# Four equal value groups of 388 columns become 512, 264, 512 and 264 in a two-layer encoder kernel

## The chip, the cores and the metric

The kernel runs on one core of a Trainium2 chip. The metric is the device time of one launch in microseconds. A core has five engines that run side by side and meet at semaphores: TensorE (PE in the profile, its weight loads as PEld) multiplies matrices into PSUM; ScalarE (ACT) and VectorE (DVE) work elementwise; GpSimd (POOL) and SyncE (SP) here mostly issue DMAs. Sixteen DMA engines move data between HBM, where the inputs lie, and SBUF, the memory that the engines read.

## What is computed

The reference is a trunk of two layers over 256 positions of width 2048. In each layer one projection feeds three groups of heads, whose gated outputs go through one output projection, a residual and a layer norm:

```python
h = x @ w_in
a_q, a_k, a_v, a_z, b_q, b_k, b_v, b_z, b_lr, m_q, m_z = jnp.split(h, cuts, axis=-1)
y_a = chunk_band_attention(heads_a(a_q), heads_a(a_k), heads_a(a_v), rel_table)   # 8 heads of 128
gate_logit = (b_lr @ gate_w + gate_b)
o_b = gla_chunk_recurrence(heads_k(b_q), heads_k(b_k), b_v, log_g)                # 4 heads, gated linear attention
y_m = memory_attention(heads_m(m_q), mk, mv)                                      # 4 heads over 256 memory tokens
y = jnp.concatenate([y_a * silu(a_z), y_b * silu(b_z), y_m * silu(m_z)], axis=-1)
return layer_norm(DEEPNORM_ALPHA * x + y @ w_out, ln_g, ln_b)
```

All inputs and outputs are float32. The change is in the part of `x @ w_in` that gives `b_lr` (16 columns), `b_v` (512) and `a_v` (1024): together 1552 columns, which the kernel calls the values.

## The kernel before

**Products.** To keep float32 accuracy at the matmul's faster format, each operand is split into a rounded part "hi" and a remainder "lo", and a product is three matmuls: hi x hi, lo x hi, hi x lo (`as_products`, L286). ScalarE makes hi by a cast (L124), VectorE makes lo by a subtraction (L125), both in `parts` (L122).

**Groups and pieces.** The projection is done in groups of columns. `as_group` (L294) takes one group of n columns: it has 2048 rows of weights, cut into 8 pieces of 2 x 128 rows. For each piece, `piece` (L136) issues the load of the raw weights into one of four buffers, makes hi and lo in one of four buffers each, and then 12 matmuls use it (2 blocks of rows, 2 halves of the positions, 3 products). They add into an accumulator in PSUM, of which there are two. So the cast of a piece can start when TensorE has finished the piece four before it, and a load can be issued when the lo part of the piece four before it has been made.

**Orders.** TensorE and SyncE run in the order in which the program is written (`manual_schedule`, L49). On ScalarE, VectorE and GpSimd the order is planned when the kernel is built, and `parts` of the weights comes first there (`high_priority(AHEAD)`, L138). All weight loads are issued by SyncE, each in its turn: an issue that has to wait holds up all that stand behind it.

**Background work.** Heads are generators that do a few small steps between the pieces. After each piece the program calls `tick` (L52) with n/512, so time is counted in pieces of 512 columns; a step that asked for 6 ticks comes when 6 have passed. GLA's steps are in `gla` (L334), those of the attention heads in `a_head` (L563), which also loads a table of biases two heads ahead (L565).

**Around the change.** In each layer the groups come in this order: queries and keys of GLA (`G_BQK`, L856), values 0 and 1 (L882, L886), in layer 0 the load of the residual input `xn`, 256 x 2048 float32 (L888), the loads of two bias tables (L893), values 2, queries and keys of attention heads 0 to 3, values 3, queries and keys of heads 4 to 7, and then the memory queries, the gates and the output projection. The four value groups have 388 columns each. They lie in `w388`, of shape (layers, 4, 8, 128, 776): for each group and piece, a partition's two rows of 388 columns lie side by side, so that a load reads 3104 bytes in one run per partition. The result goes by a copy on ScalarE (L870) into `asv`, 128 x 2 x 1552; the first 16 columns are copied on into `lr` (L884) for GLA's first step.

Other groups are loaded in two halves of 256 columns from two places; `piece` then gets a list, and issues one DMA for each entry (L144 to L147).

Of the kernel before, what the change touches and what calls it, by code (L numbers as in the profile page):

```python
# [36 lines left out]
def hybrid_trunk_kernel(  # L37
# [7 lines left out]
    pe, dve, act, pool, sp = nc.tensor, nc.vector, nc.scalar, nc.gpsimd, nc.sync  # L45
# [6 lines left out]
    def tick(share=1.0):  # L52

        now[0] += share
        for e in [e for e in side if e[1] <= now[0]]:
            side.remove(e)
            after = next(e[0], None)
            if after is not None:
                side.append((e[0], now[0] + after))
            else:  # L60
                done.add(e[0])
        while True:
            while waiting and len(active) < (3 if all(g in done for g in linear) else 2):
                active.append((waiting.pop(0), 0))
            due = [e for e in active if e[1] <= now[0]]
            if not due:
                return
            active.remove(due[0])
            g = due[0][0]
            after = next(g, None)  # L70
            if after is not None:
                active.append((g, now[0] + after))
                return
            done.add(g)

    def finish(gens):
        while not all(g in done for g in gens):
            tick()
# [18 lines left out]
    def nm(s):  # L97
        uid[0] += 1
        return f"{s}_{uid[0]}"
# [22 lines left out]
    def parts(hi, lo, src):  # L122

        act.copy(hi, src)  # L124
        dve.tensor_tensor(lo, src, hi.bitcast(F32), op=ALU.subtract)  # L125

    def load_quarter(src):

        with tc.high_priority(AHEAD):
            raw = wp.tile([P, 4, T], F32, name=nm("raw"), tag="raw")  # L130
            x = operand()
            sp.dma_start(raw, src)
            parts(x[0], x[1], raw)
        return x

    def piece(src, n, kp=2, home=None):  # L136

        with tc.high_priority(AHEAD):  # L138
            raw = wp.tile([P, kp, n], F32, name=nm("raw"), tag="raw")
            if home is None:  # L140
                hi, lo = (wp.tile([P, kp, n], F32R, name=nm(w), tag=w) for w in ("wh", "wl"))
            else:
                hi, lo = home
            if isinstance(src, list):  # L144
                w = n // len(src)
                for i, part in enumerate(src):
                    sp.dma_start(raw[:, :, i * w:(i + 1) * w], part.rearrange("p (k n) -> p k n", k=kp))  # L147
            else:
                sp.dma_start(raw.rearrange("p k n -> p (k n)"), src)
            parts(hi, lo, raw)  # L150
        return hi, lo
# [110 lines left out]
    def ws_half(src, xq):  # L262

        acc = psd.tile([P, 2, 2, T], F32, name=nm("acc"), tag="acc")
        for pc in range(4):
            wh, wl = piece(src[pc], 256, 4)
            xh, _, both = xq[pc]
            for j in range(4):
                for b in range(2):
                    mm(acc[:, b].rearrange("p h t -> p (h t)"), wh[:, j, b * P:(b + 1) * P], both[:, j], pc == j == 0, False)  # L270
                for b in range(2):
                    mm(acc[:, b, 1], wl[:, j, b * P:(b + 1) * P], xh[:, j], False, pc == j == 3)
            tick()
        return acc
# [11 lines left out]
    def as_products(o, t, xq, w, kt, kk, first=0):  # L286
        wh, wl = w
        xh, xl, _ = xq[kt // 4]
        j, ts = kt % 4, slice(t * P, (t + 1) * P)
        mm(o, xh[:, j, ts], wh[:, kk], kt == first, False)  # L290
        mm(o, xl[:, j, ts], wh[:, kk], False, False)
        mm(o, xh[:, j, ts], wl[:, kk], False, kt == 15)

    def as_group(src, xq, n, kp=2, first=None, need={}):  # L294

        acc = psd.tile([P, 2, 512], F32, name=nm("acc"), tag="acc")
        for pc in range(16 // kp):
            if first is not None and pc % 2 == 0:
                xq.append(load_quarter(first[pc // 2]))
            finish(need.get(pc, ()))  # L300
            w = piece(src[pc], n, kp)
            for kk in range(kp):
                for t in range(2):
                    as_products(acc[:, t, :n], t, xq, w, pc * kp + kk, kk)
            tick(n / 512)
        return acc
# [365 lines left out]
    def wo_pieces(l, n):  # L672

        if n < 3:
            return [w512[l, G_WO + n, pc] for pc in range(8)]
        return [[w256[l, i, pc // 2][:, pc % 2 * 512:pc % 2 * 512 + 512] for i in range(2)] for pc in range(8)]
# [141 lines left out]
    for l in range(L):  # L818
        def halves(g):
            return [[w512[l, g, h * 4 + pc // 2][:, pc % 2 * 512:pc % 2 * 512 + 512] for h in range(2)] for pc in range(8)]  # L820
# [11 lines left out]
        xq = []  # L832
# [6 lines left out]
        else:  # L839
# [4 lines left out]
            raw = hd.tile([P, 4, T], F32, name=nm("qk"), tag="qk", bufs=4)  # L844
# [5 lines left out]
        raw = hd.tile([P, 4, T], F32, name=nm("qk"), tag="qk", bufs=4)  # L850
# [15 lines left out]
        asv = per.tile([P, 2, 1552], F32, name=nm("asv"), tag="asv")  # L866

        def values(i):
            acc = as_group(w388[l, i], xq, 388)
            act.copy(asv[:, :, i * 388:(i + 1) * 388], acc[:, :, :388])  # L870

        def heads(g):
            t = hd.tile([P, 4, T], F32, name=nm("qk"), tag="qk", bufs=4)
            for i, a, b in ws_group(w512[l, g], xq):
                total(t[:, i:i + 2], a, b)
            return t
# [3 lines left out]
        lr = hd.tile([P, 2, P], F32R, name=nm("lr"), tag="qe")  # L880
        pool.memset(lr.bitcast(F32), 0.0)
        values(0)  # L882
        for i in (0, 32):
            act.copy(lr[:, :, i:i + 16], asv[:, :, :16])  # L884
        dve.tensor_tensor(lr[:, :, 16:32], asv[:, :, :16], lr[:, :, :16].bitcast(F32), op=ALU.subtract)
        values(1)  # L886
        if l == 0:
            sp.dma_start(res, xn.rearrange("(t p) d -> p t d", p=P))  # L888
# [15 lines left out]
        for half in range(2):  # L904
            values(2 + half)
            q = hd.tile([P, 4, T], F32, name=nm("qk"), tag="qk", bufs=4)
            laid = staged(G_AQ0 if half == 0 else G_AQ1, xq, yraw[3], lambda src, at, q=q: act.copy(at(q), src))
            k = heads(G_AK0 if half == 0 else G_AK1)
            finish(laid)
            gens.append([a_head(half * 4 + h, load_bias, bias, q[:, h], k[:, h], asv, yraw[1 + half][:, h]) for h in range(4)])  # L910
            waiting.extend(gens[-1])
# [6 lines left out]
        acc = as_group(halves(G_BZ), xq, 512)  # L918
# [6 lines left out]
        for i, g in ((1, G_AZ0), (2, G_AZ1), (3, G_MZ)):  # L925
            acc = as_group(halves(g), xq, 512)
# [20 lines left out]
        for n in range(WO_N):  # L947
# [3 lines left out]
            src = wo_pieces(l, n)  # L951
            if last and n == WO_N - 1:


                accs = [psd.tile([P, 2, 512], F32, name=nm("acc"), tag="acc")[:, 0], bank()]
                rest = bank()[:, :256]
                both = [operand()[2].rearrange("p (h k) n -> p h k n", h=2),
                        per.tile([P, 2, 2, 512], F32R, name=nm("late"), tag="asv")]
                homes = {pc: (x[:, 0], x[:, 1]) for pc, x in zip((2, 3), both)}
                for i, pc in enumerate((4, 5)):  # L960
                    homes[pc] = [per.tile([P, 2, 512], F32R, name=nm("late"), tag=f"yr{2 * i + k}") for k in range(2)]
                ws = [piece(src[pc], 512, 2, homes.get(pc)) for pc in range(8)]

                def products(o, t, kts, cs=slice(0, 512), first=0):
                    for kt in kts:
                        as_products(o, t, yq, [w[:, :, cs] for w in ws[kt // 2]], kt, kt % 2, first)

                products(accs[0], 0, range(16))

                def more(i):  # L970
                    if i == 0:
                        products(accs[1], 1, range(12))
                        products(accs[1][:, :256], 1, range(12, 16), slice(0, 256))
                    else:
                        products(rest, 1, range(12, 16), slice(256, 512), 12)

                norm_last(accs, rest, stats, gb, rows, more)
                break
# [4 lines left out]
            for m, pc in order:  # L983
                finish(need.pop(pc, ()))
                w = piece(wo_pieces(l, m)[pc], 512)
# [103 lines left out]
```

## Time and profile before

| | us |
|---|---|
| median of 3 runs | 907.38 (907.1 to 908.11) |
| the profiled execution | 907.3 |
| its span, first to last instruction | 905.5 |
| TensorE busy | 898.8 |
| VectorE busy | 605.4 |
| ScalarE busy | 480.3 |
| GpSimd busy | 176.0 |

The span is 1.8 us shorter than the time of its own execution, the rest lying before the first and after the last instruction. The mean clock granted to TensorE is 0.999 of full speed.

In rows of instructions the profile gives the line, the engine, the operation, the tiles it writes and reads, shapes (partitions x elements), a count, the busy time, the mean of one in ns, and the idle time of the engine before them with what ended it. A row in order of time starts with the start and the length in us; neighbours of the same kind are merged, with their count behind the x. SPq is SyncE's queue of DMA issues. Rows by stretch give, for a window of time, its length, the busy time of PE, PEld, DVE, ACT and POOL, the granted clock, the mean busy share of the DMA engines and GB/s. A row of DMA issues gives count, size of one and the median time from issue to landing.

### The profile page before, as it was taken

The page shows a single profiled execution, that of the slowest core. Times are in us where ns is not written, and L with a number is a line of the kernel's source. Part 1 is how long each engine was busy: PE and PEld are TensorE (multiplying, and loading weights), DVE is VectorE, ACT ScalarE, POOL GpSimd, SP SyncE. Part 2 cuts the span into 40 slices and gives each one's busy share as a digit, 9 for nine tenths or more (in the row PEclk, how much of TensorE's full clock was granted, in tenths as well). Part 3 has the DMA queues.
Part 4 walks back from the last instruction along what each step waited for, and adds up shares of the span by engine and source line. Part 5 has one row for each costly group of instructions (what it writes and reads, how often), then busy time and mean ns, then how long its engine had stood idle before and what let it go on. Part 6 is the DMA issues. An engine that isn't in the chain of part 4 may idle for free.

```text
span 905.5 us, 13967 instructions
## 1 busy us (share of the span) xinstructions
PE 898.8 (99%) x4926; PEld 773.8 (85%) x4926; DVE 605.4 (67%) x878; ACT 480.3 (53%) x695; POOL 176.0 (19%) x329
## 2 busy tenths in 40 slices
PE   9999999999999999999999999999999999999997
PEld 8889998998888888888888899889888888888885
DVE  6765478757566676565587676885756586766766
ACT  6654475474544656433466445754745365744440
POOL 0002002015043543200000220021141433334000
PEclk9999999999999999999999999999999999999999
DMA  9977876668787988776775686666696879889752
GB/s 313 319 214 216 299 219 194 182 205 268 216 245 206 275 260 274 225 263 188 232 250 168 202 245 204 198 194 202 192 287 195 261 209 277 253 232 280 232 164 93
DMA packets 131512, 207.16 MB, mean 229 GB/s; under 512 B 14313, under 2 KB 99689, under 8 KB 131185
## 3 DMA queue, kind: packets, MB, share of 16 engines
q1 hardware_dynamic: 117744, 173.28, 61.3%
q0 software_dynamic: 13408, 32.59, 13.1%
q8 instruction: 38, 0.62, 0.3%
q10 hardware_dynamic: 288, 0.39, 0.1%
q14 instruction: 34, 0.27, 0.1%
HBM read 189.93 MB, written 16.25 MB: 228 GB/s over the span
## 4 chain that ended last, share of the span: by engine, by line
PE 99%; DMA 0%; DVE 0%; ACT 0%; issue 0%
PE acc L102 90%; PE bk L102 8%; PE bk L648 0%; DMA raw<-w 0%; PE bk L419 0%; ACT res L804 0%; DVE stats L789 0%; PE bk L366 0%; DVE res L788 0%; ACT wh L124 0%; DVE res L740 0%; DVE mvt L743 0%; PE bk L792 0%; ACT nparts L124 0%; DVE rs_u L751 0%
## 5 line engine op out<-in xcount | busy, mean ns | idle before, releaser
L102 PE MATMUL acc<-wh,x 128*128 128x512 f32 (+2 forms) x2196 | 656.2, 380 | 0.2 <-ACT wh L124 0.2
L125 DVE TENSOR_TENSOR wl<-raw,wh 128x1024 fp32r<-128x1024 f32 (+3 forms) x321 | 368.0, 1151 | 190.2 <-ACT wh L124 188.5
L124 ACT CAST wh<-raw 128x1024 fp32r<-128x1024 f32 (+3 forms) x321 | 318.8, 995 | 320.2 <-PE acc L102 256.4
L102 PEld LDWEIGHTS acc<-wh,x 128*128 128x128 f32 x2196 | 405.5, 188 | 63.4 <-ACT wh L124 0.5
L102 PE MATMUL acc<-wl,x 128*128 128x512 f32 (+2 forms) x1098 | 414.7, 378 | 0.0
L102 PEld LDWEIGHTS acc<-wl,x 128*128 128x128 f32 x1098 | 205.9, 188 | 34.0 <-DVE wl L125 0.4
L556 POOL DMA_DIRECT2D home<-sc x58 | 32.5, 561 | 494.3 <-DVE sc L554 483.9
L102 PE MATMUL acc<-x,wh 128*128 128x512 f32 x288 | 91.1, 398 | 0.0
L102 PEld LDWEIGHTS acc<-x,wl 128*128 128x128 f32 x288 | 54.1, 188 | 12.6
L559 POOL DMA_DIRECT2D pT<-home x96 | 52.6, 554 | 41.4 <-DMA home<-sc 26.7
L102 PE MATMUL acc<-x,wl 128*128 128x256 f32 x288 | 56.7, 278 | 0.0
L102 PEld LDWEIGHTS acc<-x,wh 128*128 128x128 f32 x288 | 44.8, 189 | 1.3 <-ACT wh L124 0.2
L559 POOL DMA_DIRECT2D zT<-home x48 | 26.2, 553 | 32.8 <-DMA home<-sc 17.6
L559 POOL DMA_DIRECT2D yr<-home x48 | 26.1, 551 | 16.2 <-DMA home<-sc 7.9
L554 DVE STREAM_TRANSPOSE sc<-sc 128x512 f32<-128x512 f32 (+1 forms) x36 | 22.6, 642 | 1.9 <-ACT sc L931 1.4
L578 ACT ACTIVATE sc<-sc,mx 128x128 f32<-128x128 f32 (+1 forms) x32 | 14.4, 449 | 17.2 <-DVE mx L576 17.2
L538 DVE TENSOR_TENSOR sc<-zT,yr 128x256 f32<-128x256 f32 x24 | 8.9, 415 | 21.3 <-DMA zT<-home 21.3
L408 ACT ACTIVATE sc<-sc 128x512 f32<-128x512 f32 x12 | 7.6, 633 | 14.9 <-DVE sc L406 14.9
L124 ACT CAST x<-sc 128x512 fp32r<-128x512 f32 x20 | 11.8, 617 | 7.0 <-DVE sc L538 5.7
L571 DVE SCALAR_TENSOR_TENSOR sc<-bk,bias 128x384 f32<-128x384 f32 x16 | 8.7, 543 | 9.5 <-PE bk L102 9.5
L554 DVE STREAM_TRANSPOSE sc<-acc 128x512 f32<-128x512 f32 x18 | 11.8, 693 | 3.6 <-PE acc L102 2.8
L559 POOL DMA_DIRECT2D qk<-home x24 | 13.1, 553 | 5.0 <-DMA home<-sc 5.0
(211 smaller groups left out, 587.5 us busy)
## 6 DMA issues: line engine op xcount, KB each, us to landing
raw<-w SPq DMA_DIRECT2D x323, 256.0 KB, 4.2
raw<-w SPq DMA_DIRECT2D x94, 512.0 KB, 4.9
raw<-w SPq DMA_DIRECT2D x64, 388.0 KB, 3.5
home<-sc POOLq DMA_DIRECT2D x42, 256.0 KB, 4.4
bias<-relw SPq DMA_DIRECT2D x16, 192.0 KB, 4.6
yr<-home POOLq DMA_DIRECT2D x48, 64.0 KB, 4.7
home<-sc POOLq DMA_DIRECT2D x16, 192.0 KB, 3.2
pT<-home POOLq DMA_DIRECT2D x64, 48.0 KB, 4.2
```

Of the source, the lines that this page charges most:

```text
L102: pe.matmul(o, l, r, start=start, stop=stop, skip_group_check=True)
L124: act.copy(hi, src)
L125: dve.tensor_tensor(lo, src, hi.bitcast(F32), op=ALU.subtract)
L408: act.activation(dd, dd, AF.Abs)
L538: dve.tensor_tensor(o, z, r, op=ALU.mult)
L554: dve.transpose(blocks.rearrange("p b (g j) -> p g b j", j=32), src.rearrange("p (g b j) -> p g b j", b=4, j=32))
L556: pool.dma_start(homes[-1], blocks)
L559: pool.dma_start(dst[b * 32:(b + 1) * 32], home[:, b].rearrange("(a i) n -> i a n", a=4))
L571: dve.scalar_tensor_tensor(s, pb[:, :384], SCALE, bias[h], op0=ALU.mult, op1=ALU.add)
L578: act.activation(s[:, own[t]], s[:, own[t]], AF.Exp, bias=mx[:, t:t + 1], accum_out=zs[:, t:t + 1])
```

## The change

The 1552 columns of values are computed in groups of 512, 264, 512 and 264 columns instead of four of 388. The arrays in HBM stay as they are. Groups 0 and 1 (and 2 and 3) share the columns of two neighbouring arrays: the wide one takes all 388 columns of the first and 124 of the second, with two DMAs a piece, and the narrow one takes the other 264 of the second, with one. The runs of these loads are 1552, 496 and 1056 bytes, two per partition, instead of one of 3104. `piece` now takes lists whose entries have different widths. The number of matmuls, casts and subtractions stays; their widths change. `tick` gets 512/512 and 264/512 in place of 388/512.

```diff
             if isinstance(src, list):
-                w = n // len(src)
-                for i, part in enumerate(src):
-                    sp.dma_start(raw[:, :, i * w:(i + 1) * w], part.rearrange("p (k n) -> p k n", k=kp))
+                at = 0
+                for part in src:
+                    if len(part.shape) == 2:
+                        part = part.rearrange("p (k n) -> p k n", k=kp)
+                    sp.dma_start(raw[:, :, at:at + part.shape[2]], part)
+                    at += part.shape[2]
...
         def values(i):
-            acc = as_group(w388[l, i], xq, 388)
-            act.copy(asv[:, :, i * 388:(i + 1) * 388], acc[:, :, :388])
+            def part(j, pc, c0, c1):
+                return w388[l, j, pc].rearrange("p (k n) -> p k n", k=2)[:, :, c0:c1]
+
+            j, n = i // 2 * 2, (512, 264)[i % 2]
+            src = [[part(j + 1, pc, 124, 388)] if i % 2 else [part(j, pc, 0, 388), part(j + 1, pc, 0, 124)] for pc in range(8)]
+            acc = as_group(src, xq, n)
+            c0 = j * 388 + i % 2 * 512
+            act.copy(asv[:, :, c0:c0 + n], acc[:, :, :n])
```

## The prediction

> **What bounds the kernel now.** I read the first page for the busy engine and the chain that ended last, then the list of waits, then the order of time of TensorE, ScalarE, VectorE and SyncE around the value groups, and last the DMA share there.
>
> ```profile
> span 905.5 us, 13967 instructions
> PE 898.8 (99%) x4926; PEld 773.8 (85%) x4926; DVE 605.4 (67%) x878; ACT 480.3 (53%) x695; POOL 176.0 (19%) x329
> PE 99%; DMA 0%; DVE 0%; ACT 0%; issue 0%
> ACT wh L124 <- PE acc L102: 256.4, 184, 4.0
> ACT wh L124 <- DMA raw<-w: 22.5, 24, 4.2
> PEld bk L102 <- issue: 2.2, 8, 0.4
> ```
>
> TensorE is busy 99% of the span and is 99% of the chain: every nanosecond added to or taken from its stream shows in the time. The casts of the weights on ScalarE mostly wait for TensorE to give a buffer back (256.4 us), seldom for a load (22.5 us in 24 waits); so loads run ahead. The longest of those few, 4.2 us, is the place that matters below.
>
> I write V0 to V3 for the four value groups and V1.3 for piece 3 of V1, counting pieces from 0. There are four buffers for each of raw, hi and lo. So the cast of a piece starts when TensorE has finished the piece four before it, and a load is issued when VectorE has made the lo part of the piece four before it.
>
> **The matmuls.** A piece is 12 matmuls, a group 96, before and after. First and last rows of runs without other work in between:
>
> ```profile
> 71.68 0.52 PE L102 MATMUL acc<-wh,x 128*128 128x388 f32 x2
> 88.64 0.52 PE L102 MATMUL acc<-wh,x 128*128 128x388 f32 x2
> 105.60 0.52 PE L102 MATMUL acc<-wh,x 128*128 128x388 f32 x2
> 122.98 0.63 PE L102 MATMUL acc<-wh,x 128*128 128x512 f32 x2
> 130.48 0.62 PE L102 MATMUL acc<-wh,x 128*128 128x512 f32 x2
> 892.80 0.40 PE L102 MATMUL bk<-wh,x 128*128 128x256 f32 x2
> 895.32 1.88 PE L102 MATMUL bk<-res,ident 128*128 128x512 f32 x4
> ```
>
> V0 runs from 71.68 to 88.64 and V1 to 105.60: 16.96 us for 96, 0.1767 us a matmul of 388 columns. From 122.98 to 130.48 there are 33 of 512 columns: 0.2273 us. From 892.80 to 895.32 there are 21 of 256: 0.120 us. 264 columns are not in the trace. Between 256 and 388 the line gives 0.120 + 8/132 x 0.0567 = 0.1234 us, and I take that, 256 being the nearest row. Lower bound: 0.120, as for 256. Upper bound: the line from 512 through 388 carried on, 0.1261. A pair costs 0.2273 + 0.1234 = 0.3507 us for 2 x 0.1767 = 0.3533 before; there are 384 pairs (96 x 2 x 2 layers): **-1.0 us**, between -2.3 and 0.
>
> **The parts that cost nothing.** The cast and the lo part by width:
>
> ```profile
> L125 DVE TENSOR_TENSOR wl<-raw,wh 128x1024 fp32r<-128x1024 f32 x248 | 300.7, 1218 | 137.7 <-ACT wh L124 136.6 <-PE acc L102 0.2
> L124 ACT CAST wh<-raw 128x1024 fp32r<-128x1024 f32 x248 | 259.7, 1050 | 239.3 <-PE acc L102 188.4 <-issue 22.3 <-DMA raw<-w 14.5
> L125 DVE TENSOR_TENSOR wl<-raw,wh 128x776 fp32r<-128x776 f32 x64 | 61.7, 965 | 50.4 <-ACT wh L124 50.1
> L124 ACT CAST wh<-raw 128x776 fp32r<-128x776 f32 x64 | 54.0, 843 | 76.7 <-PE acc L102 68.0 <-DMA raw<-w 4.4 <-issue 4.0
> L125 DVE TENSOR_TENSOR wl<-raw,wh 128x512 fp32r<-128x512 f32 x7 | 4.8, 692 | 2.0 <-ACT wh L124 1.8
> L124 ACT CAST wh<-raw 128x512 fp32r<-128x512 f32 x7 | 4.4, 622 | 2.4 <-DMA raw<-w 1.9
> ```
>
> A wide piece has 1024 elements a partition: 1.05 us on ScalarE, 1.22 on VectorE. A narrow one has 528: 0.622 + 16/264 x 0.221 = 0.635, and 0.692 + 16/264 x 0.273 = 0.709. Together 1.69 and 1.93 us, for 1.69 and 1.93 now. A wide piece gives TensorE 2.73 us of work, a narrow one 1.48, and each engine stays inside that. The loads ask for 512 KB in 2.73 us and 264 KB in 1.48: 192 and 183 GB/s, for 187 now. 32 more DMA issues (8 pieces x 2 wide groups x 2 layers) on SyncE, some 0.45 us each by the row of two bias loads below; a wide piece then has two issues in 2.73 us, as every piece loaded in two halves has today, and the loads queued behind them have three pieces of cover. The copy of V0 into asv, and lr from it, come 4.8 us later; lr is first used after V2.0, over 10 us on. The planner counts n/512 a piece, 12.125 for two groups before and after, so the steps of the heads move by at most two pieces; TensorE waits nowhere over 0.4 us for them now.
>
> **The part that costs.** In layer 0 the 2048 KB load of xn stands on SyncE between the loads of V1 and of V2, and nothing passes it:
>
> ```profile
> 90.91 0.43 SPq L888 DMA_DIRECT2D res<-xn  x1
> 91.39 0.93 SPq L893 DMA_DIRECT2D bias<-relw  x2
> 92.65 6.69 SPq L149 DMA_DIRECT2D raw<-w  x4
> 88.66 0.84 ACT L124 CAST wh<-raw 128x776 fp32r<-128x776 f32 x1 [1.27 <-PE acc L102]
> 97.14 0.84 ACT L124 CAST wh<-raw 128x776 fp32r<-128x776 f32 x1 [1.27 <-PE acc L102]
> 102.21 0.84 ACT L124 CAST wh<-raw 128x776 fp32r<-128x776 f32 x1 [4.22 <-DMA raw<-w]
> 89.54 0.97 DVE L125 TENSOR_TENSOR wl<-raw,wh 128x776 fp32r<-128x776 f32 x1 [1.15 <-ACT wh L124]
> 103.08 2.92 DVE L125 TENSOR_TENSOR wl<-raw,wh 128x776 fp32r<-128x776 f32 x3 [4.10 <-ACT wh L124]
> 93.00:98.00 5.00, 5.00 (x31) 5.00 (x29) 1.93 (x2) 2.44 (x3) 0.00 (x0) 1.00 1.00 412
> 99.00:103.00 4.00, 4.00 (x25) 4.00 (x24) 0.00 (x0) 0.79 (x1) 0.00 (x0) 1.00 1.00 396
> 103.00:104.50 1.50, 1.50 (x10) 1.50 (x9) 1.39 (x2) 1.23 (x3) 0.00 (x0) 1.00 0.08 33
> 8.00:12.00 4.00, 4.00 (x21) 3.10 (x20) 3.53 (x7) 3.19 (x7) 0.00 (x0) 1.00 1.03 360
> raw<-w SPq DMA_DIRECT2D x64, 388.0 KB, 3.5
> res<-xn SPq DMA_DIRECT2D x1, 2048.0 KB, 9.2
> ```
>
> Now: V1 starts at 88.64, which frees a buffer for V1.3: cast 88.66, lo part 89.54 to 90.51, and behind it SyncE issues V1.7 and, at 90.91, xn. The DMA engines are full (share 1.00) from 93 to 103 and then empty (0.08): xn, two biases, then V2.0 to V2.3. xn lands after 9.2 us. V2.0, issued at 92.65, takes until 102.2, where such a piece lands after 3.5 us in the median: it stands behind xn. Its cast, due one piece (2.12 us) after V1.7's at 97.14, starts at 102.21, 11.30 us after xn's issue. Its lo part ends at 104.05; TensorE needs V2.0 from 105.60 on. So 1.5 us are left today: the late load is hidden, just.
>
> After: V0 takes 96 x 0.2273 = 21.82 us, so V1 starts at 93.50. From there to xn's issue it was 90.91 - 88.64 = 2.27 us; the narrow cast and lo part take 0.46 off: 1.81, so xn goes out at 95.31, 4.40 later than now. V2.0's cast follows it by 11.30 plus what the larger piece adds. 512 for 388 KB is 0.32 us more at 396 GB/s; at the 360 GB/s of a stretch of shorter rows it is 0.46, which I take: 102.21 + 4.40 + 0.46 = 107.07. Cast until 108.12, lo part until 109.34. But V1 is narrow: 96 x 0.1234 = 11.85 us, so TensorE is through with it at 105.35, and its third matmul of V2.0, the first to read the lo part, was due at 105.80. **It waits 3.5 us.** V2.1 lands some 1.4 us after V2.0 and is ready near 111; it is wanted at 112: one wait. Bounds: from the end of V2.0's bytes (the first of four in 99 to 103, so 100.0) to its cast now stand 2.2 us; were they nothing, 1.3 us of wait remain. Should V2.0 move at half of 396 GB/s, 4.4 us.
>
> [...]
>
> Sum: -1.0 + 3.5 = +2.5 us on the profiled execution's 907.3, so **909.8**. The median of the runs, 907.38, is the same within 0.1 us. This case's own range is 908.0 to 911.3, short of the bounds of both terms falling together (906.3 and 911.7).
>
> **Rivals.** *The load is hidden anyway (0.20).* The completion could come sooner in the new order; it decides from a cast of V2.0 at 103.5 (105.80 less 1.05 and 1.22), 3.6 us sooner than I work out. For it: the loads are ahead nearly everywhere. Against: SyncE issues in order, and xn's issue hangs on V1's start. Then only the columns count: 907.3 - 1.0 = 906.3, or 905.0 at their lower bound.
>
> *TensorE's clock falls in the gap (0.15).*
>
> ```profile
> 900.04 0.62 PE L102 MATMUL bk<-gbrow,nparts 4*128 4x512 f32 x2
> 902.00:903.00 1.00, 0.00 (x0) 0.00 (x0) 0.00 (x0) 0.00 (x0) 0.00 (x0) 0.97 1.02 375
> 903.00:904.00 1.00, 0.00 (x0) 0.00 (x0) 0.00 (x0) 0.00 (x0) 0.00 (x0) 0.50 0.43 154
> ```
>
> At the end the granted clock drops to 0.50 near 902.9, 2.3 us after the last matmul ended at 900.66; the new gap is empty from 105.35 to 108.12, 2.8 us. [...] Half speed lasted at least the 2.5 us to the end of the span; as long here, it costs 1.3 us: 911.1. [...]
>
> *Narrow pieces give too little cover elsewhere (0.09).* While TensorE runs narrow pieces, wide ones are prepared, in V1 and V3 of both layers: three pieces of 1.48 us, 4.4, against 1.05 + 1.22. Beyond 2.2 us of delay on ScalarE or VectorE by heads' work TensorE waits. One us in each of the three other places: 912.8. Against: casts and lo parts are planned first, and layer 1 loads no xn.
>
> *264 columns cost like 388 (0.03).* 384 x 0.053 is 20 us: 930. The 256-column row speaks against it.
>
> **How the numbers follow.** My case has 0.53. I count 0.2% (1.8 us) as what a measurement can tell from no change. Three quarters of my case lie above 909.2: 0.39, with 0.15, 0.09 and 0.03 that is 0.66 slower. A quarter of it, 0.14, and half of the hidden case, 0.10, stay within: 0.24. Faster is the other half, 0.10, with the columns at their lower bound. The range, 905.8 to 912.8, leaves out the last rival and parts of the hidden and the third.
>
> **What would show it.** One TensorE gap of 2 to 3.5 us near 105 in layer 0, ended by the cast and lo part of V2.0, which itself waits for its load some 7 us; xn's issue near 95.3; nothing like it in layer 1; 264-column matmuls 0.120 to 0.126 us apart; the clock at 1.00 through 105 to 115. I am wrong if V2.0's cast begins by 103.5, if layer 1 or the stretch after V3 also shows a gap, or if the 264-column matmuls are further apart.

## The result, and the profile after

The changed kernel takes 913.75 us (median of 6 runs, 911.51 to 917.02), the kernel before, measured beside it, 907.33 (907.02 to 908.64): a ratio of 1.0068 [1.0054, 1.0082] (in brackets, here and below, the 95% interval). It is slower, and its time lies 0.95 us above the top of the predicted range. The profiled execution took 913.23 us; before it was 907.3. Two executions among all runs below, one of the narrow groups first and one of the filled gap, took over 990 us at a mean granted clock of 0.85, and no number below counts them.

The first page of the profile after; the last line is the chain of work that ended last:

```profile
span 911.4 us, 14041 instructions
PE 899.6 (99%) x4926; PEld 758.5 (83%) x4926; DVE 608.2 (67%) x878; ACT 479.9 (53%) x695; POOL 176.0 (19%) x329
PE 95%; DMA 2%; DVE 1%; ACT 1%; issue 1%; SPq 0%; POOL 0%; ACTq 0%; DVEq 0%
```

The span is 5.9 us longer with the same 4926 matmuls. TensorE's share of the chain fell from 99% to 95%; a load, ScalarE and VectorE now stand in it. Its new waits, as total, count and longest in us:

```profile
PE acc L102 <- ACT wh L124: 3.1, 2, 2.9
PE bk L102 <- DVE sc L125: 0.8, 1, 0.8
PE bk L102 <- DVE mq L125: 0.7, 1, 0.7
PE bk L102 <- ACT sc L124: 0.4, 1, 0.4
PE acc L102 <- DVE wl L125: 0.4, 1, 0.4
```

None of these was there before beyond 0.2 us; three others, of 1.1, 0.3 and 0.3 us, are the same before and after. The first and the last of the list belong to one place, the start of V2 in layer 0 (0.2 us of the first apart). In order of time on TensorE (the change moves later line numbers by 3 or 9):

```profile
71.65 0.62 PE L102 MATMUL acc<-wh,x 128*128 128x512 f32 x2
93.41 0.40 PE L102 MATMUL acc<-wh,x 128*128 128x264 f32 x2
104.86 0.28 PE L102 MATMUL acc<-wl,x 128*128 128x264 f32 x1
108.07 0.85 PE L102 MATMUL acc<-wh,x 128*128 128x512 f32 x2 [2.92 <-ACT wh L124]
109.33 0.79 PE L102 MATMUL acc<-wl,x 128*128 128x512 f32 x1 [0.41 <-DVE wl L125]
112.92 0.38 PE L369 MATMUL bk<-ident,lr 128*128 128x128 f32 x2
```

and on SyncE, ScalarE and VectorE:

```profile
95.38 0.60 SPq L897 DMA_DIRECT2D res<-xn  x1
106.97 1.04 ACT L124 CAST wh<-raw 128x1024 fp32r<-128x1024 f32 x1 [1.19 <-DMA raw<-w]
108.05 1.23 DVE L125 TENSOR_TENSOR wl<-raw,wh 128x1024 fp32r<-128x1024 f32 x1 [7.40 <-ACT wh L124]
```

V0 takes 21.76 us (71.65 to 93.41). V1 takes 11.57: its last matmul begins at 104.86, and a matmul of 264 takes 0.12, so TensorE could go on at 104.98. V2.0's cast begins only at 106.97, behind a load, and its lo part ends at 109.28. The third matmul, due two matmuls of 512 after 104.98, at 105.43, begins at 109.33: **3.9 us of waiting for the load**. V2.0's matmuls are over only at 112.92, where the head's step at L369 begins: 3.59 us for 10 of them, more than their 2.27 at the former rate. The granted clock (last column but two) says why:

```profile
108.00:109.00 1.00, 0.85 (x2) 0.30 (x2) 0.95 (x1) 0.54 (x2) 0.00 (x0) 0.76 1.06 348
109.00:110.00 1.00, 0.67 (x2) 0.58 (x3) 0.72 (x2) 0.59 (x2) 0.00 (x0) 0.50 0.49 146
110.00:111.00 1.00, 1.00 (x4) 0.81 (x3) 0.78 (x1) 0.97 (x1) 0.00 (x0) 0.50 0.45 78
111.00:112.00 1.00, 1.00 (x3) 0.76 (x3) 1.00 (x1) 0.62 (x1) 0.00 (x0) 0.54 0.91 321
112.00:113.00 1.00, 1.00 (x6) 0.78 (x5) 0.23 (x1) 0.43 (x1) 0.00 (x0) 1.00 1.16 203
```

What is missing to full clock is 0.24 + 0.50 + 0.50 + 0.46 = 1.70 us; at half speed that is 3.4 us, from about 108.5 to 111.9. It costs the **1.3 us** by which those 10 matmuls are longer. The place costs 5.2 us in all.

The other three waits are steps of the heads that read the memory tokens, near 358 in layer 0 and near 739 in layer 1:

```profile
357.63 0.50 PE L102 MATMUL bk<-sc,mv 128*128 128x256 f32 x2 [0.42 <-ACT sc L124]
358.95 0.75 PE L102 MATMUL bk<-sc,mv 128*128 128x256 f32 x4 [0.82 <-DVE sc L125]
739.58 0.50 PE L102 MATMUL bk<-mk,mq 128*128 128x256 f32 x2 [0.67 <-DVE mq L125]
357.00 1.23 DVE L125 TENSOR_TENSOR wl<-raw,wh 128x1024 fp32r<-128x1024 f32 x1 [1.36 <-PE acc L102]
358.14 0.75 DVE L125 TENSOR_TENSOR sc<-pT,sc 128x256 fp32r<-128x256 f32 x2
```

The same steps in the kernel before ran without an entry for a wait, but not with much to spare (the row of VectorE is the lo part of mq that the second of these two steps needs):

```profile
350.00 0.89 PE L102 MATMUL bk<-sc,mv 128*128 128x256 f32 x6
730.49 0.88 PE L102 MATMUL bk<-mk,mq 128*128 128x256 f32 x6
730.08 0.68 DVE L125 TENSOR_TENSOR mq<-yr,mq 128x512 fp32r<-128x512 f32 x1
```

After, VectorE takes a weight's lo part from 357.00 to 358.23 ahead of the head's own two, so TensorE waits. Counted from one start of a matmul to the next, beyond the usual distance, the three cost 0.58, 0.98 and 0.83: **2.4 us**.

Where no wait intervenes the columns give time back: V0 and V1 together took 33.92 us before (71.68 to 105.60) and 33.33 now. Taken for all four such pairs of groups that is -2.4 us. So -2.4 + 5.2 + 2.4 = +5.2 of the span's 5.9; 0.7 us has no place in this sum. Some 0.3 of it is at the heads' steps, where the matmul behind a wait takes longer too: from the matmul before to the one behind, against the same stretch before, they cost 1.75 and 0.91, 2.7 in all.

### The profile page after: what moved, and what is told of

The parts are those of the page before. It is cut to its first block, busy times and chain, and to the rows that moved or that the text cites. A ratio compares the mean times of both kernels' runs of the same rounds, so it can differ in the third digit from the quotient of the medians.

```text
span 911.4 us, 14041 instructions
## 1 busy us (share of the span) xinstructions
PE 899.6 (99%) x4926; PEld 758.5 (83%) x4926; DVE 608.2 (67%) x878; ACT 479.9 (53%) x695; POOL 176.0 (19%) x329
## 4 chain that ended last, share of the span: by engine, by line
PE 95%; DMA 2%; DVE 1%; ACT 1%; issue 1%; SPq 0%; POOL 0%; ACTq 0%; DVEq 0%
PE acc L102 87%; PE bk L102 7%; DMA raw<-w 1%; DMA yr<-home 1%; ACT wh L124 0%; PE bk L651 0%; DVE wl L125 0%; POOL yr L562 0%; SPq L149 0%; SPq L902 0%; PE bk L422 0%; DVE sc L125 0%; ACT res L807 0%; DVE mq L125 0%; DVE mx L579 0%
## 5 line engine op out<-in xcount | busy, mean ns | idle before, releaser
L102 PEld LDWEIGHTS acc<-wh,x 128*128 128x128 f32 x2196 | 400.7, 188 | 76.5 <-ACT wh L124 3.6
```

The lines of the kernel that those rows point to most:

```text
L102: pe.matmul(o, l, r, start=start, stop=stop, skip_group_check=True)
```

## The experiments

The first theory: V2.0 comes late because V1 now starts later, and xn's issue with it, while V1 is shorter; the clock falls because of that gap; and the heads' waits come from a third thing, the background steps falling on other pieces. The rivals: the loads in two parts are slow by themselves; the clock would have fallen anyway, or costs more than its place in one profile shows; narrow pieces give too little cover wherever they stand. Each ratio below is to the kernel before, run on the same chip.

**xn's load behind V2's.** Nothing is then ahead of V2.0.

```diff
         values(1)
-        if l == 0:
-            sp.dma_start(res, xn.rearrange("(t p) d -> p t d", p=P))
...
             values(2 + half)
+            if l == half == 0:
+                sp.dma_start(res, xn.rearrange("(t p) d -> p t d", p=P))
```

> The changed kernel with one move: in layer 0 the load of xn stands behind the loads of V2 instead of ahead of them. My theory (V2.0 stands behind xn in SyncE's order, and the narrow V1 both starts later and ends sooner): the gap at V2.0 is gone, the clock stays at 1.00 there, and the 5.2 us lost between 105.0 and 112.9 come back: 908.0 from the profiled 913.2, the two waits for memory heads (2.4 us) being still there. Rival, a narrow group gives too little cover whatever is loaded: a gap of 1 us or more stays at V2.0, 909 to 911.

Measured: 906.81 us (906.04 to 910.41), 0.9991 [0.9981, 1.0001]. In order of time on ScalarE and TensorE:

```profile
101.71 1.05 ACT L124 CAST wh<-raw 128x1024 fp32r<-128x1024 f32 x1 [1.88 <-DMA raw<-w]
104.91 0.62 PE L102 MATMUL acc<-wh,x 128*128 128x512 f32 x2
107.66 0.38 PE L369 MATMUL bk<-ident,lr 128*128 128x128 f32 x2
```

V2.0's cast is 5.3 us sooner, TensorE goes straight on at 104.91, and L369 is reached 5.26 us sooner than in the changed kernel. One head's wait of 0.6 us is left near 352. The loss against the kernel before goes with the place of one DMA. It goes further than the theory said, which had 908.0: of the heads' 2.4 us of waits only 0.6 are left, although the ticks are those of the change. So these waits depend on more than the ticks; by what way xn's place acts on them is not shown.

**The same, and the ticks of before.** Each value piece counts 388/512 again, so that the heads' steps fall on the pieces on which they fell before.

```diff
-    def as_group(src, xq, n, kp=2, first=None, need={}):
+    def as_group(src, xq, n, kp=2, first=None, need={}, share=None):
...
-            tick(n / 512)
+            tick(share or n / 512)
...
-            acc = as_group(src, xq, n)
+            acc = as_group(src, xq, n, share=388 / 512)
```

> As the kernel with xn behind V2, and the planner counts each piece of a value group as 388/512 as before, so that every step of the heads stands behind the same piece as before the change. If the two waits of TensorE for memory heads come from the moved steps, they vanish: 905.3 (907.3 less 2.0 for the columns). Rival, they come from the order that the planner finds for ScalarE, VectorE and GpSimd once widths differ: they stay or move elsewhere, 907 to 908.

Measured: 906.17 us (905.14 to 907.9), 0.9982 [0.9972, 0.9992]: faster than before by 0.2%, with an interval that leaves out 1. TensorE's whole list of waits:

```profile
PE bk L102 <- DVE eps L820: 1.1, 1, 1.1
PE bk L102 <- ACT nparts L124: 0.3, 1, 0.3
PE bk L795 <- DVE nt L757: 0.3, 1, 0.3
```

These three stand in the profile of before too, so this run shows the gain of the columns alone: its span is 903.4 us, 2.1 less than before.

**The ticks alone**, with xn where the change has it.

> The changed kernel, xn where it was, with 388/512 counted for each value piece, so that the heads' steps stand behind the same pieces as before the change. The wait for V2.0 in layer 0 and its fall of the clock stay (5.2 us), the waits for memory heads go if the moved steps made them: 907.3 - 2.0 + 5.2 = 910.5. Rival, those waits have nothing to do with the steps' places: 912 to 914, with a gap near 357 or 738.

Measured: 912.31 us (911.38 to 912.95), 1.0049 [1.0032, 1.0065].

```profile
108.83 0.88 PE L102 MATMUL acc<-wh,x 128*128 128x512 f32 x2 [3.00 <-ACT wh L124]
109.00:110.00 1.00, 0.71 (x2) 0.12 (x2) 1.00 (x1) 0.78 (x1) 0.00 (x0) 0.63 1.06 349
```

The wait at V2.0 and the half clock behind it are still there, the heads' waits are not: the first loss does not need the second. Against the change the ratio is lower by 0.0019, 1.7 us, where 2.4 us were counted, and the two intervals overlap. The median lies above the 910.5 expected and in the rival's 912 to 914; the rival's gaps near 357 and 738 are not in the profile, whose execution took 911.38.

**Half of xn ahead of V2, half behind.** If the bytes ahead of V2.0 are the cause, half of them make half the delay.

```diff
-        if l == 0:
-            sp.dma_start(res, xn.rearrange("(t p) d -> p t d", p=P))
+        def load_xn(t):
+            if l == 0:
+                sp.dma_start(res[:, t], xn[t * P:(t + 1) * P])
+
+        load_xn(0)
...
             values(2 + half)
+            if half == 0:
+                load_xn(1)
```

> The changed kernel with half of xn (1024 KB) between the loads of V1 and V2 and the other half behind V2's loads. If the wait is the time that V2.0 stands behind xn's bytes, it falls by 1.05 MB at 412 GB/s, 2.5 us: from 3.9 to 1.4 us, and a gap this short leaves the clock at 1.00: 913.2 - 2.5 - 1.3 = 909.4. Rival, it is the order or the latency of one more load, not its bytes: the wait stays near 3.9 and the time near 913.

Measured: 909.17 us (908.21 to 915.4), 1.0013 [0.9994, 1.0032].

```profile
104.72 1.05 ACT L124 CAST wh<-raw 128x1024 fp32r<-128x1024 f32 x1 [4.80 <-DMA raw<-w]
105.82 0.73 PE L102 MATMUL acc<-wh,x 128*128 128x512 f32 x2 [0.67 <-ACT wh L124]
107.08 0.51 PE L102 MATMUL acc<-wl,x 128*128 128x512 f32 x1 [0.53 <-DVE wl L125]
109.49 0.38 PE L369 MATMUL bk<-ident,lr 128*128 128x128 f32 x2
```

The cast is 2.25 us sooner than in the changed kernel. The wait shrinks from 3.9 us to about 1.6, and the clock stayed at 1.00 (107.08 to 109.49 is 2.4 us for the 10 matmuls that took 3.59). The delay goes with the bytes that stand ahead.

**The change in V0 and V1 alone** (V2 and V3 are 388 wide as before), **and in V2 and V3 alone.** The edit of the first is shown; the second has 1 in place of 0.

```diff
         def values(i):
+            if i // 2 != 0:
+                acc = as_group(w388[l, i], xq, 388)
+                act.copy(asv[:, :, i * 388:(i + 1) * 388], acc[:, :, :388])
+                return
```

> Only V0 and V1 are 512 and 264 wide; V2 and V3 stay at 388. V2.0 is smaller (cast some 0.4 us sooner, 0.84 and 0.97 us for cast and lo part): TensorE waits about 3.1 us for it instead of 3.9, columns give 1.0 back: 909.4 with a full clock, 910.7 if it falls for 3.4 us. No waits for memory heads, since the steps behind V2 and V3 are where they were. Rival, V2 must be wide for a wait: 906.3.

Measured: 912.23 us (911.24 to 913.58), 1.0046 [1.0032, 1.0061].

```profile
107.47 0.62 PE L102 MATMUL acc<-wh,x 128*128 128x388 f32 x2 [2.41 <-ACT wh L124]
108.47 0.69 PE L102 MATMUL acc<-wl,x 128*128 128x388 f32 x1 [0.38 <-DVE wl L125]
109.00:110.00 1.00, 1.00 (x5) 1.00 (x4) 1.00 (x2) 0.88 (x2) 0.00 (x0) 0.50 0.52 127
```

> Only V2 and V3 are 512 and 264 wide. V2.0, now the larger, is cast near 102.6 and ready at 104.9, TensorE wants it at 105.6: no wait. Columns give 1.0 back, waits for memory heads may cost 0 to 2.4 as the steps move: 906.3 to 908.7. Rival, the narrow V3 starves the wide group after it: a gap of 1 us or more near 192 or 640, and above 909.

Measured: 909.21 us (907.66 to 911.84), 1.0014 [1.0004, 1.0024].

```profile
103.52 1.05 ACT L124 CAST wh<-raw 128x1024 fp32r<-128x1024 f32 x1 [4.83 <-DMA raw<-w]
354.30 0.74 PE L102 MATMUL bk<-sc,mv 128*128 128x256 f32 x4 [0.82 <-DVE sc L125]
735.78 0.51 PE L102 MATMUL bk<-mk,mq 128*128 128x256 f32 x2 [0.97 <-DVE mq L125]
```

The first pair brings the wait at V2.0 and the half clock, with V2 itself unchanged: what matters is when V1 starts and ends. The second pair brings two of the heads' waits, and no wait at V2.0: its cast begins at 103.52 and the lo part is done at 105.83, while V1 ends at 106.30 there and the first matmul that reads the lo part begins at 106.76. Each pair alone is slower than before; neither gain of columns pays. Both medians lie above what was expected (910.7 and 908.7 at most); what the other 1.5 and 0.5 us are, these profiles don't say.

**The loads in one run.** The same group widths from arrays packed by width, so that a wide piece is one DMA with a single run of 4096 bytes a partition, and no row of 496 bytes is left. The lines that pack the arrays are not shown.

```diff
-            src = [[part(j + 1, pc, 124, 388)] if i % 2 else [part(j, pc, 0, 388), part(j + 1, pc, 0, 124)] for pc in range(8)]
+            src = (wv512, wv264)[i % 2][l, i // 2]
```

> The changed kernel with its value weights laid out in two arrays by width, so that each piece is one load of one run per partition (4096 or 2112 bytes) in place of runs of 1552, 496 and 1056 bytes. My theory, it is the place behind xn and not the form of the load: V2.0 is cast some 0.3 us sooner (106.7 for 106.97) and the time changes by less than 1 us. Rival, the short runs and the second issue make V2.0 late: its cast comes 2 us sooner or more, and the time falls to 911 or below.

Measured: 912.56 us (912.0 to 913.89), 1.0051 [1.0036, 1.0066]. On SyncE, ScalarE and TensorE, and a row by stretch:

```profile
95.76 0.43 SPq L894 DMA_DIRECT2D res<-xn  x1
107.48 1.04 ACT L124 CAST wh<-raw 128x1024 fp32r<-128x1024 f32 x1 [1.10 <-DMA raw<-wv]
108.58 0.73 PE L102 MATMUL acc<-wh,x 128*128 128x512 f32 x2 [2.84 <-ACT wh L124]
110.00:111.00 1.00, 1.00 (x4) 0.82 (x5) 1.00 (x1) 1.00 (x1) 0.00 (x0) 0.73 0.45 70
```

The cast comes not 0.3 us sooner, as its author estimated, but 0.5 later; xn went out 0.4 later too. From xn's issue to V2.0's cast are 11.72 us, for 11.59 with two DMAs a piece. The form of the loads is not the cause. Taking the rows of 496 bytes away shortened nothing here.

**The gap filled.** Useless matmuls on the identity stand between V1 and V2 in layer 0 and cover the wait; they add work and change no output. The profile shows the 12 as 24.

```diff
+        if l == 0:
+            idle = bank()
+            for _ in range(12):
+                mm(idle[:, :P], ident, ident, True, True)
```

> The changed kernel with 12 matmuls of no use (128 columns, some 0.22 us each, 2.6 us) between V1 and V2 in layer 0, in the gap. If the clock fell because of the gap: V2.0 still comes at the same time, but the granted clock stays at 1.00 and 1.3 us or more come back, 909 to 912, and the runs lie closer together than 911.5 to 917.0. Rival, the fall of the clock has another cause or costs nothing: 913 to 914 with the same spread.

Measured: 910.32 us (909.32 to 910.99), 1.0027 [1.0016, 1.0039].

```profile
105.08 2.84 PE L102 MATMUL bk<-ident 128*128 128x128 f32 x24
109.30 0.50 PE L102 MATMUL acc<-wl,x 128*128 128x512 f32 x1 [0.53 <-DVE wl L125]
111.72 0.38 PE L369 MATMUL bk<-ident,lr 128*128 128x128 f32 x2
110.00:112.00 2.00, 2.00 (x12) 1.60 (x11) 1.75 (x2) 1.62 (x2) 0.00 (x0) 1.00 0.68 225
```

V2.0's cast, at 106.94, and its third matmul come as late as in the changed kernel (106.97, 109.33). But the clock stays at 1.00 and L369 is reached at 111.72 instead of 112.92, 1.2 us sooner. So the fall of the clock is a consequence of the empty TensorE, and it is worth 1.2 us at its place. Of the ratios, 1.0068 and 1.0027, the difference is 3.7 us; the heads' waits differ too between the two kernels (one of 1.5 us here), so the rest isn't assigned. The runs lie closer together, as expected: 909.32 to 910.99, for 911.51 to 917.02.

**Narrow groups first**: 264, 512, 264, 512 columns, so that V1 is the wide group and V2.0 a narrow piece.

```diff
-            j, n = i // 2 * 2, (512, 264)[i % 2]
-            src = [[part(j + 1, pc, 124, 388)] if i % 2 else [part(j, pc, 0, 388), part(j + 1, pc, 0, 124)] for pc in range(8)]
+            j, n = i // 2 * 2, (264, 512)[i % 2]
+            src = [[part(j, pc, 264, 388), part(j + 1, pc, 0, 388)] if i % 2 else [part(j, pc, 0, 264)] for pc in range(8)]
...
-            c0 = j * 388 + i % 2 * 512
+            c0 = j * 388 + i % 2 * 264
```

> Widths 264, 512, 264, 512, xn where it was. V1 is then wide: it starts near 83.3, xn goes out near 86, V2.0 is cast near 97.5 and TensorE wants it near 105. My theory: no gap at V2.0, clock 1.00 throughout, 905.3 to 908 by how many waits for heads there are. Rival, a narrow group next to a wide one starves TensorE by itself: gaps of 1 us or more at V1.0 and V3.0 or after, above 909.

Measured: 907.84 us (907.03 to 909.07), 1.0001 [0.9991, 1.001]. The profile is that of a second run of the same kernel:

> Widths 264, 512, 264, 512 once more, for a profile at full clock. It took as long as the kernel before, 2 us more than the columns let expect. If that is waits for memory heads, as in the changed kernel, gaps of 0.5 us or more stand near 350 or 735, in sum 1 to 2 us, and none at V1.0, V2.0 or V3.0. Rival, narrow groups starve TensorE: gaps at the group borders.

Measured: 908.65 us (905.34 to 910.35), 0.9999 [0.998, 1.0018]. On SyncE and ScalarE of the profiled execution, which took 905.34:

```profile
91.88 0.59 SPq L897 DMA_DIRECT2D res<-xn  x1
103.43 0.64 ACT L124 CAST wh<-raw 128x528 fp32r<-128x528 f32 x1 [5.82 <-DMA raw<-w]
```

xn goes out 3.5 us sooner than in the changed kernel (95.38) and TensorE isn't held up at V2.0, nor at any head: the order of the widths decides. Yet the profiled execution is the quickest of eight, and the others take 2 to 5 us longer for something that a profile of this one can't show. In some of them a part lies outside the span: the time is up to 2.9 us longer than the span, where in all runs of the other kernels it is 1.7 to 1.9. The rest stays open. That xn would go out near 86 was wrong: V1's first casts wait up to 3.0 us for their own loads, wide ones asked for while narrow pieces are used up, and xn's issue follows them.

**Control: the kernel before with xn's load behind V2's**, the first experiment's edit made there.

> The kernel before, all groups at 388 columns, with the load of xn behind V2's loads. My theory: the late V2.0 was covered there, so nothing changes, within 0.2%. Rival, the place of xn is worth something by itself: 905.5 or less.

Measured: 908.4 us (907.61 to 909.28), 0.9996 [0.9981, 1.0011]. Moving xn is worth nothing that this run can tell where TensorE doesn't wait behind it. What the first experiment won, it won back from the change.

**Everything together**: packed arrays, xn behind V2, the ticks of before.

> All that has helped so far together: widths 512 and 264 from arrays packed by width, xn behind V2, steps of the heads where they were. No wait at V2.0, none for the memory heads, the columns' 2 us kept: 905.5 to 906.2 where the kernel before takes 907.5 to 908, a ratio near 0.998. Rival, the loads' short runs cost elsewhere too: 905 or less.

Measured: 906.32 us (905.13 to 907.0), 0.9971 [0.9957, 0.9986]: the fastest ratio of all, and faster than both kernels. Packing adds nothing beyond the intervals (0.9982 without). One wait in its profile speaks against too simple a story of the heads:

```profile
284.70 0.50 PE L102 MATMUL bk<-mk,mq 128*128 128x256 f32 x2 [0.85 <-DVE mq L125]
```

With the ticks as before a head's step can still be late. The ticks explain the heads' waits of most kernels here (none in three of the four with the old ticks or the old second pair, some in six of the seven others that were read in the profile), not of all.

## Why the prediction was wrong

**The wait for V2.0, +3.5: right in mechanism and nearly in size, 3.9.** xn's issue was put at 95.31 and came at 95.38; V2.0's cast at 107.07, came at 106.97; the lo part's end at 109.34, came at 109.28. The 0.4 us is V1's end, 104.98 in place of 105.35. That it is xn's place in the queue, and V1's start and length, is shown by moving xn (the wait goes), by halving it (1.6 us), by the first pair alone (it stays) and by the control. The prediction's bound of 4.4 us comes to 4.7 by its own figures (512 KB at 198 GB/s is 1.64 us more than 388 KB at 396, not 1.32); nothing hangs on it. Half of 396 GB/s was its author's estimate, and the profile after doesn't show it: between 104 and 109, with V2.0 on its way, the DMA engines moved 348 to 369 GB/s.

**The clock: a step that failed.** The price was right (1.3 us, and the filled gap gives 1.2). What failed is the chance of 0.15, and with it that the price was left out of the sum. The prediction had the row that decided, half clock 2.3 us after the last matmul of the kernel, with a gap of 2.8 us to come; that the chance was so low all the same was its author's estimate, for which no run shows a ground. The clock fell after a gap of 2.9 us, and in the first-pair kernel after one of 2.4 (as the rows of TensorE give them).

**The heads' steps, "cost nothing": wrong, and the largest error of the sum, 2.4 us in the profile.** The cover named was that TensorE waited nowhere over 0.4 us for them. That no wait is seen doesn't say how much time there is to spare: the lo part of mq was ready at 730.76 for matmuls from 730.49 on. Steps moved by a piece or two meet other weights on VectorE. The ticks alone took these waits away, and the second pair alone brought two of them; but xn's place changed them as well, and with everything together one is left. That the moved steps are the whole cause is therefore not shown. Gaps behind V3 and in layer 1 were among the prediction's own signs of being wrong; these waits are such gaps, by another way than the one it had in mind.

**The columns, -1.0: too small, -2.1 to -2.4.** 264 columns cost 0.1205 us (11.57 us for 96), nearly the 0.120 of 256 columns, the lower bound named; the line between 256 and 388 put them at 0.1234. 512 cost 0.2267 in V0 rather than 0.2273. The span of the run without new waits gives -2.1.

**The rest of the parts at nothing: right.** Cast and lo part of a narrow piece were put at 635 and 709 ns and took 634 and 708:

```profile
L124 ACT CAST wh<-raw 128x528 fp32r<-128x528 f32 x32 | 20.3, 634 | 40.9 <-PE acc L102 38.8 <-DVE res L669 2.1
```

Packed loads moved nothing beyond the intervals (1.0051 for 1.0068), so the added issues and the short rows cost nothing that can be seen. The third rival, narrow pieces that give too little cover in V3 or in layer 1, did not come: the 3.1 us of waits for a weight's hi part hold 2.9 at V2.0 and 0.2 in one other wait, as before.

With what was measured in their place the terms are -2.1 + 3.9 + 1.3 + 2.4 = +5.5: 912.8 from 907.3, for 913.23 in the profiled execution. The range took the losses one at a time: the forecast's wait, or with it the clock (911.1), with 912.8 at its top from narrow pieces elsewhere. The losses came together, with a third that no rival had, the heads' steps. That the median lies another 0.5 higher, and single runs at 917.02, goes with a mean granted clock of 0.993 to 0.997 in the six runs. The other three kernels with the long gap at V2.0 (ticks alone, first pair, packed) have 0.994 to 0.997 too; all others have 0.997 to 0.999, but for one run of half xn (0.995, 915.4 us) and one of the kernel before (0.994, 915.12 us). Those executions have no trace, so no more is said of it.

## What to carry to other kernels

When a group of work changes its length, follow what is issued at its start: here a 2 MB load left 4.5 us later and the group that hid it became 5.4 us shorter, and that decided the sign although the matmuls got cheaper. A gap of TensorE costs its length and, at the gaps of 2.4 us and more measured here, a stretch of about 3.4 us at half clock behind it, worth 1.2 to 1.3 us in the changed kernel; count both. (The longest gap looked at without a fall is one of 1.47 us, near 737 in the filled kernel, with matmuls of 512 columns 0.23 us apart behind it; between that and 2.4 us none of the gaps looked at between two matmuls stands.) That a profile shows no wait at a step is no slack: before moving it, read how long before its use its inputs are ready.

## What the hardware showed unexpectedly

The clock. After gaps of 2.41 us (first pair alone), 2.84 (packed), 2.92 (the change) and 3.00 (ticks alone), each followed by two matmuls and another short wait, it went to 0.50 and stayed there for about 3.4 us. That began some 0.4 us after TensorE had started again in the changed kernel, but 1.9 us after it in the packed one (110.46 for 108.58). In the 3.4 us ahead of the fall TensorE was busy for 0.49 us in the change, 0.43 with the ticks alone, 0.88 in the first pair and 1.35 in the packed kernel. After two waits of 0.67 and 0.53 us (half of xn; 2.2 us busy of 3.4) and where useless matmuls filled the gap, it stayed at 1.00. Behind the last matmul of a profile it fell as well, and not after the same time: before, 2.3 us after that matmul's end (900.66, near 902.9); in the changed kernel 0.6 us after it (906.62, near 907.2), where TensorE had been busy for 2.2 us of the 3.4:

```profile
906.00 0.62 PE L102 MATMUL bk<-gbrow,nparts 4*128 4x512 f32 x2
907.00:908.00 1.00, 0.00 (x0) 0.00 (x0) 0.00 (x0) 0.35 (x1) 0.00 (x0) 0.62 0.71 270
```

So neither the length of the emptiness nor the busy time ahead gives the moment of the fall by itself; what does, these runs don't show.
